# Sixteen row blocks of a down projection by seven block products in place of eight, with the weights' sums added up in DRAM by DMAs

## The chip, the cores and the metric

The kernel runs on one core of one Trainium2 chip. A core has five engines with an instruction stream each: TensorE (PE, the matmuls), VectorE (DVE), ScalarE (ACT), GpSimd (POOL) and SyncE (SP, which here issues nearly all DMAs), and 16 DMA engines that they share. The metric is the device time of one execution in microseconds (us).

## What is computed

One inference step of a hybrid layer for 512 prompt tokens (behind 16 meta tokens) and 8 x 8 sample tokens, with a model width of 1024. The end of it is what the change touches:

```python
def hybrid_layer(x, ...):
    proj = rmsnorm(x, norm1_w) @ w_in
    ...                                   # pooling mixer, conv, SSD scan, gated norm
    merged = sigmoid(g_a) * a_out + sigmoid(g_b) * b_out
    x = x + merged @ w_o
    hn2 = rmsnorm(x, norm2_w)
    up, ffn_new = causal_dwconv(hn2 @ w_up, ffn_buf, ffn_conv_w, ffn_conv_b)
    x = x + (silu(up[..., :D_FF]) * up[..., D_FF:]) @ w_down      # D_FF = 2816 = 22 * 128
    ...                                   # final rmsnorm, states
```

## The kernel before

Activations stand with features on the partitions and 576 tokens (512 and 64) along the row. Every product is one of fp32 numbers, made of three matmuls: a number is split in a high part (rounded to the fast format) and a low part (the rest), and `mm3` (L120 to L124) multiplies low weight by high activation, high by high, and high by low. Weights come by DMA (`load_w`, L95: 1 MB for two units of 128 output columns, two buffers `wr`); `split_w` makes the high part on ACT (L116) and the low part on DVE (L117), in two buffers `wh` and `wl` each.

A `Unit` is the product for 128 output columns: `split`, `product` (its matmuls into PSUM banks, three `mm` and five `px`) and `finish`, which calls the function that takes the result out. `run` goes through a list of units and splits the weights two units ahead. A scheduler then orders the instructions of each engine, so that their places are not those of the source.

The parts of the program, in order: input projection with pooling and conv (to some 190 us), the scan of the SSD mixer, woven with output products (to some 600 us), merge, the projection `w_o`, and the ConvFFN. In the scan each step loads rows of a cumulated sum from DRAM (`cumD`, L730), from which DVE makes decays (L733), and states (`state_ssm`, L814). SP issues these loads in turn with the weights' (L95), the gating rows (`gAD`, `mAD`, L625 and L629) and others. POOL clears and fills the edges of the conv's buffers (`ext`, L651 and L652; the pooling's, L544 and L545).

In the ConvFFN the 22 row blocks of the hidden width are made in pairs of units: a gate unit j and a value unit j. `ffn_conv` takes a unit out of PSUM (L1152 to L1154), convolves it (L1160 on ACT, L1162 twice on DVE); `gate_post` applies silu (L1174, L1175), `val_post` multiplies value by gate (L1185) and splits the product (L1189 on ACT, L1190 on POOL). One up unit has 48 matmuls. Units 0 to 11 are followed by `down0`, the down projection of these 12 row blocks: 8 units (128 output columns each) of 12 x 2 halves x 3 = 72 matmuls of 288 columns, added to x by DVE (L1215). Then units 12 to 21 and `last`, 8 units over 10 row blocks (60 matmuls each), woven with the output (`out_block`) and with 14 DMAs that write the FFN's states (L695).

```python
    down0 = down_units(0, [6, 6], GHALF)
    last = down_units(12, [8, 2], LAST)
    seq = up + down0 + ff_units(12, 10) + [out_begin, last[0]]
```

## Time and profile before

| | |
|---|---|
| median of 3 runs | 1235.24 us (1232.61 to 1235.53) |
| the profiled execution | 1235.61 us, span 1233.9 us |
| granted clock of TensorE | 0.996 of full speed |
| PE, DVE, ACT, POOL busy | 1216.6, 776.3, 556.0, 165.7 us |
| DMA traffic | 144.0 MB, mean 117 GB/s |

The span goes from the first to the last instruction of the profiled execution; 1.7 us of its time lie around it. Busy times are shares of this span; one engine's idle time matters only where PE waits for it.

### The profile page before, as it was taken

The page shows a single profiled execution, that of the slowest core. Times are in us where ns is not written, and L with a number is a line of the kernel's source. Part 1 is how long each engine was busy: PE and PEld are TensorE (multiplying, and loading weights), DVE is VectorE, ACT ScalarE, POOL GpSimd, SP SyncE. Part 2 cuts the span into 40 slices and gives each one's busy share as a digit, 9 for nine tenths or more (in the row PEclk, how much of TensorE's full clock was granted, in tenths as well). Part 3 has the DMA queues.
Part 4 walks back from the last instruction along what each step waited for, and adds up shares of the span by engine and source line. Part 5 has one row for each costly group of instructions (what it writes and reads, how often), then busy time and mean ns, then how long its engine had stood idle before and what let it go on. Part 6 is the DMA issues. An engine that isn't in the chain of part 4 may idle for free.

```text
span 1233.9 us, 22634 instructions
## 1 busy us (share of the span) xinstructions
PE 1216.6 (99%) x9159; PEld 1178.2 (95%) x9159; DVE 776.3 (63%) x1378; ACT 556.0 (45%) x1167; POOL 165.7 (13%) x323
## 2 busy tenths in 40 slices
PE   9999999999999999999999999999999999999996
PEld 7999999899899989989999999999999999999996
DVE  6785346669788988887643344377666325677634
ACT  6444333554567577566442224344434112434432
POOL 0340000002023013011100001221212000111100
PEclk9999999999999999999999999999999999999999
DMA  7244327651634555654553532223322223222322
GB/s 209 55 135 118 107 88 214 165 169 46 188 112 122 149 151 142 192 150 132 152 146 106 173 132 71 68 70 103 103 69 78 78 86 103 69 69 88 111 72 77
DMA packets 173432, 144.00 MB, mean 117 GB/s; under 512 B 11622, under 2 KB 162830, under 8 KB 173321
## 3 DMA queue, kind: packets, MB, share of 16 engines
q1 hardware_dynamic: 172865, 142.14, 39.4%
q8 instruction: 72, 1.18, 0.4%
q10 hardware_dynamic: 464, 0.42, 0.1%
q14 instruction: 31, 0.25, 0.1%
HBM read 122.43 MB, written 20.34 MB: 116 GB/s over the span
## 4 chain that ended last, share of the span: by engine, by line
PE 89%; DMA 4%; DVE 3%; ACT 2%; issue 1%; SPq 0%; POOL 0%; DVEq 0%; ACTq 0%; POOLq 0%
PE mm L122 26%; PE mm L123 26%; PE mm L124 26%; DMA t<-cumD 2%; PE px L785 1%; DMA t<-in_state_ssm_dram 1%; PE px L763 1%; PE px L794 1%; PE px L825 1%; DMA wr<-in_w_in_dram 1%; PE px L878 1%; PE px L838 1%; ACT t L735 1%; PE px L747 1%; DVE wl L117 1%
## 5 line engine op out<-in xcount | busy, mean ns | idle before, releaser
L122 PE MATMUL mm<-s,wl 128*128 128x288 f32 (+4 forms) x2512 | 754.9, 301 | 1.1 <-DVE wl L117 0.6
L123 PE MATMUL mm<-s,wh 128*128 128x288 f32 (+4 forms) x2512 | 746.8, 297 | 0.0
L124 PE MATMUL mm<-s,wh 128*128 128x288 f32 (+4 forms) x2256 | 671.8, 298 | 0.0
L122 PEld LDWEIGHTS mm<-s,wl 128*128 128x128 f32 x2512 | 473.8, 189 | 7.7 <-issue 5.3
L123 PEld LDWEIGHTS mm<-s,wh 128*128 128x128 f32 x2512 | 473.6, 189 | 3.6 <-issue 3.0
L124 PEld LDWEIGHTS mm<-s,wh 128*128 128x128 f32 x2256 | 424.6, 188 | 1.5 <-issue 1.4
L117 DVE TENSOR_TENSOR wl<-wr,wh 128x1024 fp32r<-128x1024 f32 (+1 forms) x164 | 197.9, 1207 | 167.0 <-ACT wh L116 166.5
L116 ACT ACTIVATE wh<-wr 128x1024 fp32r<-128x1024 f32 (+1 forms) x164 | 170.0, 1037 | 233.9 <-PE mm L124 197.1
L124 PE MATMUL mm<-t,wh 128*128 128x290 f32 (+1 forms) x256 | 75.9, 297 | 0.0
L1162 DVE SCALAR_TENSOR_TENSOR acc<-ext,ffT,acc 128x592 f32<-128x592 f32 x88 | 74.2, 844 | 1.7 <-ACT acc L1160 0.2
L663 DVE SCALAR_TENSOR_TENSOR acc<-ext,scT,acc 128x616 f32<-128x616 f32 x72 | 63.8, 886 | 0.9 <-ACT acc L661 0.4
L735 ACT ACTIVATE t<-t,TK 128x128 f32<-128x128 f32 (+1 forms) x160 | 48.4, 384 | 24.4 <-DVE t L733 24.4
L947 POOL TENSOR_TENSOR sqs<-sqs,acc 128x578 f32<-128x578 f32 x19 | 31.3, 1647 | 140.5 <-ACT acc L946 75.3
L124 PEld LDWEIGHTS mm<-t,wh 128*128 128x128 f32 x256 | 48.2, 188 | 0.0
L1189 ACT ACTIVATE s<-ext 128x512 fp32r<-128x512 f32 (+1 forms) x44 | 17.1, 436 | 64.3 <-DVE ext L1185 64.3
L882 ACT ACTIVATE t<-t,spr 128x128 f32<-128x128 f32 x128 | 40.3, 393 | 8.4 <-PE px L825 8.3
L1153 DVE TENSOR_TENSOR ext<-mm,t 128x224 f32<-128x224 f32 x43 | 16.8, 391 | 42.0 <-PE mm L124 42.0
L804 POOL TENSOR_TENSOR s<-s,tmp 128x256 f32<-128x256 f32 (+1 forms) x32 | 35.5, 1129 | 54.8 <-DVE tmp L798 47.2
L1190 POOL TENSOR_TENSOR s<-ext,s 128x512 fp32r<-128x512 f32 (+1 forms) x44 | 37.4, 870 | 35.1 <-ACT s L1189 35.1
L1215 DVE TENSOR_TENSOR t<-t,mm 128x288 f32<-128x288 f32 (+2 forms) x30 | 13.6, 452 | 43.8 <-PE mm L124 43.6
L1160 ACT ACTIVATE acc<-ext,ffT 128x592 f32<-128x592 f32 x44 | 38.2, 870 | 1.6 <-DVE ext L1154 1.6
L1156 POOL COPY t<-ext 128x18 f32<-128x18 f32 x44 | 11.4, 258 | 203.1 <-DVE ext L1154 203.0
(292 smaller groups left out, 1289.5 us busy)
## 6 DMA issues: line engine op xcount, KB each, us to landing
wr<-in_w_in_dram SPq DMA_DIRECT2D x29, 1024.0 KB
wr<-in_w_up_dram SPq DMA_DIRECT2D x22, 1024.0 KB
t<-cumD SPq DMA_DIRECT2D x16, 512.0 KB
t<-in_state_ssm_dram SPq DMA_DIRECT2D x32, 256.0 KB
out_dram<-t SPq DMA_DIRECT2D x32, 256.0 KB
wr<-in_w_ssd_out_dram SPq DMA_DIRECT2D x8, 1024.0 KB
wr<-in_w_down_dram SPq DMA_DIRECT2D x8, 768.0 KB
wr<-in_w_down_dram SPq DMA_DIRECT2D x8, 640.0 KB
```

Of the source, the lines that this page charges most:

```text
L116: S.activation(wh[:, :kb, :n], wr, AF.Copy)
L117: V.tensor_tensor(wl[:, :kb, :n], wr, f(wh[:, :kb, :n]), ALU.subtract)
L122: PE.matmul(o, wl[:, k, :m], hi[:, a:b], start=first, stop=False)
L123: PE.matmul(o, wh[:, k, :m], hi[:, a:b], start=False, stop=False)
L124: PE.matmul(o, wh[:, k, :m], lo[:, a:b], start=False, stop=last)
L663: V.scalar_tensor_tensor(acc[:, 0:616], ext[:, k:k + 616], scT[:, kb, 24 + k:25 + k], acc[:, 0:616], op0=ALU.mult, op1=ALU.add)
L735: S.activation(seg[:q, h, :q], seg[:q, h, :q], AF.Exp, scale=-1.0, bias=sums_[:, h:h + 1])
L804: G.tensor_tensor(v, v, t1[:, 2 * i:2 * i + 2, :nt], ALU.add)
L882: S.activation(v[:, b], v[:, b], AF.Copy, scale=elS[:, 4 * u + 2 * i + b, 4 * g + j:4 * g + j + 1])
L1160: S.activation(acc[:, 0:w], ext[:, 0:w], AF.Identity, scale=ffT[:, kb, 16:17], bias=ffT[:, kb, 19:20])
L1162: V.scalar_tensor_tensor(acc[:, 0:w], ext[:, k:k + w], ffT[:, kb, 16 + k:17 + k], acc[:, 0:w], op0=ALU.mult, op1=ALU.add)
L1190: G.tensor_tensor(l, a, f(h), ALU.subtract)
```

## The change

Row blocks 0 to 15 of `w_down` are taken in two groups of eight. In a group, the row blocks are read as four even and four odd ones, the output columns as two halves of four blocks each, and the tokens as two halves of 288. That is a 2 x 2 by 2 x 2 product of blocks, made by seven products (Winograd's form of Strassen's method) in place of eight. Four of the seven take sums of weight blocks, S1 to S4, and four take differences of the gated rows, N1, N2, T3 and T4.

`Sums` makes S1 to S4 of each group in DRAM: four DMAs on SP (L196) copy a block of the weights, [4, 128, 512] of 1 MB, and seven DMAs on POOL (L202) add another one to it. In the source they are woven into the merge (group 0) and the up projection (group 1). `Parts` loads the weights of four products (4 x 256 KB, L225). A `Two` is a unit of two products, 2 x 4 x 3 = 24 matmuls of 288 columns each, with one px bank a product; a group is 14 of them. `seven_post` adds a product to its one, two or three places in x. `val_post` makes the differences and their parts for every second row block below 16. The value rows' scale `rs2` moves to another buffer. Row blocks 16 to 21 stay in `last`, with 36 matmuls a unit. The first up unit of the next group now stands between the group's last value unit and its first `Two`.

```diff
--- before.py
+++ after.py
@@ -139,7 +139,7 @@
                 wr = self.raw() if callable(self.raw) else load_w(*self.raw)
                 self.ws, k0 = [], 0
                 for kb in self.kbs:
-                    w = split_w(wr[:, k0:k0 + kb, self.at:self.at + self.n], kb, self.n, self.spare if kb == 2 else None)
+                    w = split_w(wr[:, k0:k0 + kb, self.at:self.at + self.n], kb, self.n, self.spare if kb <= 2 else None)
                     self.ws += [(w, k) for k in range(kb)]
                     k0 += kb
                 self.pss = []
@@ -174,6 +174,106 @@
             else:
                 self.post(self.pss)
             due[:0] = [fn() for fn in now]
+    SEVEN = (("A11", "B11"), ("A12", "B21"), ("S4", "B22"), ("S2", "N2"), ("S1", "N1"), ("S3", "T3"), ("A22", "T4"))
+    class Sums:
+        def __init__(self, src, k0, name):
+            rows = src[k0 * 128:(k0 + 8) * 128, :].rearrange("(k e p) c -> e k p c", e=2, p=128)
+            self.at = {f"A{i + 1}{e + 1}": rows[e][:, :, 512 * i:512 * i + 512] for i in range(2) for e in range(2)}
+            self.d = {s: dp.tile([4, 128, 512], F32, name=f"{name}{s}") for s in ("S1", "S2", "S3", "S4")}
+        def copies(self):
+            def go(s, a):
+                return lambda: DMA.dma_start(out=self.d[s], in_=self.at[a])
+            return [go("S4", "A12"), go("S2", "A11"), go("S1", "A21"), go("S3", "A11")]
+        def adds(self):
+            def go(s, a):
+                return lambda: G.dma_start(out=self.d[s], in_=self.at[a], accum_op=ALU.add)
+            return [go("S4", "A11"), go("S2", "A21"), go("S1", "A22"), go("S3", "A21"), go("S4", "A21"), go("S2", "A22"), go("S4", "A22")]
+        def steps(self):
+            c, a = self.copies(), self.adds()
+            return [c[0], c[1], a[0], c[2], a[1], c[3], a[4], a[2], a[5], a[3], a[6]]
+        def view(self, name, mp):
+            full = self.d[name] if name in self.d else self.at[name]
+            return full.rearrange("k p c -> p k c")[:, :, 128 * mp:128 * mp + 128]
+    class Parts:
+        def __init__(self, views):
+            self.views, self.of, self.nxt = views, None, None
+        def load(self):
+            if self.of is None:
+                raws.clear()
+                self.of = wp.tile([128, 4, 4, 128], F32, tag="wr", bufs=2, name=nm("wr"))
+                for i, v in enumerate(self.views):
+                    DMA.dma_start(out=self.of[:, i], in_=v)
+        def get(self, i):
+            self.load()
+            if self.nxt:
+                self.nxt.load()
+            return self.of[:, i]
+    class Two(Unit):
+        def __init__(self, prods):
+            Unit.__init__(self, None, 0, None, None, None, None)
+            self.prods = prods
+        def split(self):
+            if self.ws is None:
+                self.ws = []
+                wh = wp.tile([128, 2, 4, 128], F32R, tag="wh", bufs=WBUFS, name=nm("wh"))
+                wl = wp.tile([128, 2, 4, 128], F32R, tag="wl", bufs=WBUFS, name=nm("wl"))
+                for i, (parts, at, *_) in enumerate(self.prods):
+                    src, n = parts.get(at), 4
+                    S.activation(wh[:, i, :n], src, AF.Copy)
+                    V.tensor_tensor(wl[:, i, :n], src, f(wh[:, i, :n]), ALU.subtract)
+                    self.ws.append(((wh[:, i], wl[:, i]), n))
+        def product(self, halves=None, piece=None):
+            for (_, _, acts, post), (w, n) in zip(self.prods, self.ws):
+                ps = px_tile()
+                for k in range(n):
+                    act = acts(k)
+                    n2 = act[0].shape[1]
+                    mm3(ps[:, :n2], w, k, 128, act, 0, n2, k == 0, k == n - 1)
+                post(ps)
+        def finish(self):
+            for fn in due:
+                fn()
+            due.clear()
+            now = pend[:]
+            pend.clear()
+            due[:0] = [fn() for fn in now]
+    def seven_units(sums, mps, acts, post):
+        todo = [(mp, w, x) for mp in mps for w, x in SEVEN]
+        parts = [Parts([sums.view(w, mp) for mp, w, _ in todo[i:i + 4]]) for i in range(0, len(todo), 4)]
+        for a, b in zip(parts, parts[1:]):
+            a.nxt = b
+        prods = [(parts[i // 4], i % 4, lambda k, x=x: acts(k)[x], lambda ps, mp=mp, w=w: post(mp, w, ps))
+                 for i, (mp, w, x) in enumerate(todo)]
+        return [Two(prods[i:i + 2]) for i in range(0, len(prods), 2)]
 
     def run(seq, nxt_units=()):
 
@@ -1131,14 +1231,17 @@
 
     o_units = mat_units(w_o_m, 0, [8], 2, lambda: [(blk(mh, k), blk(ml, k)) for k in range(KD)], ALIVE, o_post)
     o_units[0].k_outer = True
-    run(merge[:2] + [ff_params] + merge[2:] + [lambda: xr.extend(load_x(c) for c in range(5))], o_units)
-    x2s = []
+    dsum = [Sums(w_dn_m, 8 * i, f"w{i}") for i in range(2)]
+    run(merge[:2] + [ff_params] + weave(merge[2:], dsum[0].steps()) + [lambda: xr.extend(load_x(c) for c in range(5))], o_units)
+    x2s, rs2 = [], []
 
     def x2_norm():
-        return rnorm(sums["n2"], DM, lambda r, a, b: S.activation(rs2[:, a:b], r, AF.Copy))
-    nff, rs2 = slot([128, 18 * 44]), slot([128, NA])
+        spread = rnorm(sums["n2"], DM, lambda r, a, b: S.activation(rs2[0][:, a:b], r, AF.Copy))
+        rs2.append(ep.tile([128, NA], F32, tag="sqs", bufs=1, name=nm("sqs")))
+        return spread
+    nff = slot([128, 18 * 44])
 
     LF = LP - A0
     WF = LF + 8 * NB
...
@@ -1175,19 +1277,60 @@
         V.scalar_tensor_tensor(ext[:, 0:w], ext[:, 0:w], 1.0, acc[:, 0:w], op0=ALU.add, op1=ALU.mult)
         gates[j] = ext
 
+    NH = NY // 2
+    gB, quad = {}, {}
+    gh, gl = [], []
+    def split_g(hi, lo, src, eng):
+        S.activation(hi, src, AF.Copy)
+        eng.tensor_tensor(lo, src, f(hi), ALU.subtract)
     def val_post(j, pss):
-        if j % 2 == 0:
-            gh.extend(pairs(2, F32R))
-            gl.extend(pairs(2, F32R))
         _, acc, w = ffn_conv(NF + j, pss)
-        t = gates.pop(j)
-        for a, b in zip(parts(t), parts(acc)):
-            V.tensor_tensor(a, a, b, ALU.mult)
-        hi, lo = blk(gh, j)[:, :NY], blk(gl, j)[:, :NY]
-        for a, h, l in zip(parts(t), (hi[:, 0:NP], hi[:, NP:].rearrange("p (b j) -> p b j", b=NB)),
-                           (lo[:, 0:NP], lo[:, NP:].rearrange("p (b j) -> p b j", b=NB))):
-            S.activation(h, a, AF.Copy)
-            G.tensor_tensor(l, a, f(h), ALU.subtract)
+        t, p, e = gates.pop(j), j // 2, j % 2
+        if j >= 16:
...
+            return
+        if e == 0:
+            quad[p] = slot([128, 4, NH])
+        qd = quad[p]
+        g = qd[:, 2 * e:2 * e + 2].rearrange("p h t -> p (h t)")
+        for o, a, b in zip((g[:, 0:NP], g[:, NP:].rearrange("p (b j) -> p b j", b=NB)), parts(t), parts(acc)):
+            V.tensor_tensor(o, a, b, ALU.mult)
+        if e == 0:
+            new = slot if p % 4 == 3 else big
+            gB[p] = [new([128, 4, NH], F32R), new([128, 4, NH], F32R), big([128, 4, NH], F32R),
+                     gB[p - 1][3] if p % 2 else big([128, 4, NH], F32R)]
+            split_g(gB[p][2][:, 0], gB[p][2][:, 2], qd[:, 0], G)
+            return
+        del quad[p]
+        n1, n2 = t[:, 0:NH], t[:, NH:2 * NH]
+        t3, t4 = qd[:, 1], acc[:, 0:NH]
+        split_g(gB[p][0][:, 0:2], gB[p][1][:, 0:2], qd[:, 2:4], G)
+        V.tensor_tensor(n1, qd[:, 0], qd[:, 1], ALU.subtract)
+        V.scalar_tensor_tensor(n2, n1, -1.0, qd[:, 3], op0=ALU.mult, op1=ALU.subtract)
+        V.tensor_tensor(t3, qd[:, 3], qd[:, 1], ALU.subtract)
+        V.scalar_tensor_tensor(t4, n2, -1.0, qd[:, 2], op0=ALU.mult, op1=ALU.subtract)
+        split_g(gB[p][0][:, 2:4], gB[p][1][:, 2:4], t[:, 0:2 * NH].rearrange("p (h t) -> p h t", h=2), V)
+        split_g(gB[p][2][:, 1], gB[p][2][:, 3], t3, V)
+        i = 2 * (p % 2)
+        split_g(gB[p][3][:, i], gB[p][3][:, i + 1], t4, V)
+    def g_ops(p):
+        a, b, c, d = gB[p]
+        i = 2 * (p % 2)
+        return dict(B21=(a[:, 0], b[:, 0]), B22=(a[:, 1], b[:, 1]), N1=(a[:, 2], b[:, 2]), N2=(a[:, 3], b[:, 3]),
+                    B11=(c[:, 0], c[:, 2]), T3=(c[:, 1], c[:, 3]), T4=(d[:, i], d[:, i + 1]))
 
     def ff_units(j0, nj):
         out = []
@@ -1254,20 +1397,53 @@
             if q < n:
                 S.dma_start(out=o_ys.rearrange("b j d -> (b j) d"), in_=y[q:n, :])
 
-    def down_units(j0, kbs, halves):
-        return mat_units(w_dn_m, j0, kbs, 1, lambda: [(blk(gh, j0 + k), blk(gl, j0 + k)) for k in range(sum(kbs))], halves,
+    held = {}
+    def seven_post(mp, w, ps):
+        def to(c, src, op):
+            o = blk(x2, mp + 4 * (c // 2))[:, NMETA + NH * (c % 2):NMETA + NH * (c % 2) + NH]
+            V.tensor_tensor(o, o, src, op)
+        p = ps[:, :NH]
+        if w == "A11":
+            u = held["u"] = acc_tile()[:, :NH]
+            S.activation(u, p, AF.Copy)
+            to(0, p, ALU.add)
+        elif w == "S2":
+            u = held["u"]
+            V.tensor_tensor(u, u, p, ALU.add)
+            to(2, u, ALU.subtract)
+        elif w == "S1":
+            u = held.pop("u")
+            V.tensor_tensor(u, u, p, ALU.add)
+            to(1, u, ALU.add)
+            to(3, u, ALU.subtract)
+        elif w == "S3":
+            to(2, p, ALU.subtract)
+            to(3, p, ALU.subtract)
+        else:
+            c = {"A22": 2, "S4": 1, "A12": 0}[w]
+            to(c, p, ALU.subtract if c == 2 else ALU.add)
+    def down_sevens(i):
+        return seven_units(dsum[i], range(4), lambda k: g_ops(4 * i + k), seven_post)
+    def down_units(kbs, halves):
+        return mat_units(w_dn_m, 16, kbs, 1, lambda: [(blk(gh, k), blk(gl, k)) for k in range(6)], halves,
                          lambda m, pss: down_post(m, halves, pss))
 
-    up = ff_units(0, 12)
+    up = ff_units(0, 8)
     x_turn(0)
     run(o_units, up)
     x2s += [(blk(x2h, k), blk(x2l, k)) for k in range(KD)]
     pend.append(x2_norm)
     up[0].late, up[1].new, up[0].k_outer = True, px_tile, True
-    down0 = down_units(0, [6, 6], GHALF)
-    last = down_units(12, [8, 2], LAST)
+    up2, up3 = ff_units(8, 8), ff_units(16, 6)
+    last = down_units([5, 1], LAST)
     last[0].mate, last[1].mates, last[1].new = last[1], True, px_tile
-    seq = up + down0 + ff_units(12, 10) + [out_begin, last[0]]
+    seq = (weave(up, dsum[1].steps()) + up2[:1] + down_sevens(0) + up2[1:] + up3[:1] + down_sevens(1) + up3[1:]
+           + [out_begin, last[0]])
     for m in range(1, 6):
         seq += [last[m], *([ff_states] if m == 2 else []), lambda m=m: out_block(0, m - 1), lambda m=m: out_block(1, m - 1)]
     run(seq, last[6:])
```

Where the scheduler puts the DMAs of the sums is seen on SP and POOL. First SP, before, at the start of the scan, around the load of cumD into t310 (`wr` are weights, t308 and t309 states):

```order
L629 DMA mAD_139<-ext294_2356 128x578
L95 DMA wr330_2651<-in_w_pool_out_dram 128x8x256
L814 DMA t308_2464<-in_state_ssm_dram 128x4x128 x2
L814 DMA t309_2467<-in_state_ssm_dram 128x4x128 x2
L629 DMA mAD_139<-ext304_2453 128x578
L730 DMA t310_2470<-cumD_118 128x1024
L625 DMA ext329_2646<-gAD_140 128x578
```

The same place now; w1S1 is the second group's S1:

```order
L729 DMA mAD_139<-ext294_2356 128x578
L196 DMA w1S1_7486<-in_w_down_dram 512x1x512
L729 DMA mAD_139<-ext304_2453 128x578
L914 DMA t308_2464<-in_state_ssm_dram 128x4x128 x2
L914 DMA t309_2467<-in_state_ssm_dram 128x4x128 x2
L830 DMA t310_2470<-cumD_118 128x1024
L729 DMA mAD_139<-ext317_2548 128x578
L725 DMA ext329_2646<-gAD_140 128x578
```

The copy w1S1 has come ahead of the states and of t310's cumD, and the weight load wr330 has gone behind them. The other seven copies stand on SP between the early weight loads and the next step of the scan.

On POOL, before, in the pooling and the first conv buffers:

```order
L544 MEMSET ext133_1002 128x15
L545 COPY ext133_1002<-t19_113 128x8x15
L550 COPY t20_138<-ext133_1002 128x15
L551 COPY t20_138<-ext133_1002 128x64
L544 MEMSET ext150_1098 128x15
L545 COPY ext150_1098<-t19_113 128x8x15
L550 COPY t20_138<-ext150_1098 128x15
L551 COPY t20_138<-ext150_1098 128x64
L651 MEMSET ext161_1175 128x3
L652 COPY ext161_1175<-scT_115 128x8x3
```

And now:

```order
L644 MEMSET ext133_1002 128x15
L645 COPY ext133_1002<-t19_113 128x8x15
L202 DMA w0S4_7485<-in_w_down_dram 512x1x512
L650 COPY t20_138<-ext133_1002 128x15
L651 COPY t20_138<-ext133_1002 128x64
L644 MEMSET ext150_1098 128x15
L645 COPY ext150_1098<-t19_113 128x8x15
L650 COPY t20_138<-ext150_1098 128x15
L651 COPY t20_138<-ext150_1098 128x64
L202 DMA w0S4_7485<-in_w_down_dram 512x1x512
L751 MEMSET ext161_1175 128x3
L752 COPY ext161_1175<-scT_115 128x8x3
```

Two adds to w0S4 have come in between; the second waits for the first one's end, and ext161's clearing stands behind it. The other twelve follow further on, to the middle of the scan.

On DVE, before, behind the last value unit ahead of `down0`, from one split of `down0`'s weights (wl1309) to the next:

```order
L117 TENSOR_TENSOR wl1309_10742<-wr1305_10735,wh1308_10741 128x768
L1162 SCALAR_TENSOR_TENSOR acc1313_10801<-ext1312_10795,ffT_602,acc1313_10801 128x592 x2
L1185 TENSOR_TENSOR ext1303_10723<-ext1303_10723,acc1313_10801 128x512
L1185 TENSOR_TENSOR ext1303_10723<-ext1303_10723,acc1313_10801 128x8x8
L117 TENSOR_TENSOR wl1316_10814<-wr1314_10811,wh1315_10813 128x768
```

And now, where the first group of sevens begins, from the splits of the first `Two` (wl1267) on:

```order
L248 TENSOR_TENSOR wl1267_10315<-wr1268_10316,wh1266_10314 128x512 x2
L1265 SCALAR_TENSOR_TENSOR acc1265_10296<-ext1264_10290,ffT_602,acc1265_10296 128x592 x2
L1255 TENSOR_TENSOR ext1272_10381<-mm1270_10331,sqs1146_9204 128x290
L1308 TENSOR_TENSOR t1249_10158<-ext1257_10221,acc1265_10296 128x512
L1308 TENSOR_TENSOR t1249_10158<-ext1257_10221,acc1265_10296 128x64
L1319 TENSOR_TENSOR ext1257_10221<-t1249_10158 128x288
L1320 SCALAR_TENSOR_TENSOR ext1257_10221<-ext1257_10221,t1249_10158 128x288
L1321 TENSOR_TENSOR t1249_10158<-t1249_10158 128x288
L1322 SCALAR_TENSOR_TENSOR acc1265_10296<-ext1257_10221,t1249_10158 128x288
L1286 TENSOR_TENSOR t1251_10162<-ext1257_10221,t1250_10161 128x576
L1286 TENSOR_TENSOR s1252_10163<-t1249_10158,s1252_10163 128x288
L1286 TENSOR_TENSOR s1222_9875<-acc1265_10296,s1222_9875 128x288
```

Between the first `Two`'s splits and the next unit's stood the conv and the gating of a value unit, and now the differences (L1319 to L1322) and three low parts (L1286) besides. The rest of the evacuation (L1256, L1257) and the splits of the second `Two` (L248) come right behind.

## Rows read from the trace of the kernel before

**Rows 1.** The page's busy times of the engines.
```profile
PE 1216.6 (99%) x9159; PEld 1178.2 (95%) x9159; DVE 776.3 (63%) x1378; ACT 556.0 (45%) x1167; POOL 165.7 (13%) x323
```

**Rows 2.** Busy time by stretch; columns: from:to, length, engines, granted clock, DMA share, GB/s.
```profile
970.00:975.00 5.00, 5.00 (x40) 5.00 (x40) 0.96 (x1) 1.07 (x2) 0.00 (x0) 1.00 0.49 142
```

**Rows 3.** DVE's timeline, down projection: start, length, line, operation [idle before].
```profile
975.13 0.96 DVE L117 TENSOR_TENSOR wl<-wr,wh 128x768 fp32r<-128x768 f32 x1 [3.81 <-ACT wh L116]
984.68 0.96 DVE L117 TENSOR_TENSOR wl<-wr,wh 128x768 fp32r<-128x768 f32 x1 [3.81 <-ACT wh L116]
```

**Rows 4.** DVE's timeline and busy times over pairs of up projection units.
```profile
932.24 1.23 DVE L117 TENSOR_TENSOR wl<-wr,wh 128x1024 fp32r<-128x1024 f32 x1 [0.57 <-ACT wh L116]
933.39 1.70 DVE L1162 SCALAR_TENSOR_TENSOR acc<-ext,ffT,acc 128x592 f32<-128x592 f32 x2
937.56 0.39 DVE L1153 TENSOR_TENSOR ext<-mm,t 128x224 f32<-128x224 f32 x1 [0.84 <-PE mm L124]
938.65 1.23 DVE L117 TENSOR_TENSOR wl<-wr,wh 128x1024 fp32r<-128x1024 f32 x1 [0.57 <-ACT wh L116]
941.78 0.82 DVE L1185 TENSOR_TENSOR ext<-ext,acc 128x512 f32<-128x512 f32 x2
...
918.35:943.96 25.61, 25.61 (x194) 25.61 (x193) 17.82 (x30) 10.28 (x14) 4.66 (x13) 1.00 0.23 67
```

**Rows 5.** Groups by line and shape: busy time, mean ns of one, idle before.
```profile
L117 DVE TENSOR_TENSOR wl<-wr,wh 128x768 fp32r<-128x768 f32 x16 | 15.7, 978 | 28.0 <-ACT wh L116 28.0
L117 DVE TENSOR_TENSOR s<-wr,s 128x256 fp32r<-128x256 f32 x9 | 4.6, 506 | 11.8 <-ACT s L116 11.8
L1215 DVE TENSOR_TENSOR t<-t,mm 128x288 f32<-128x288 f32 x16 | 7.3, 454 | 19.0 <-PE mm L124 18.8
L1077 DVE TENSOR_TENSOR acc<-acc,ext 128x288 f32<-128x288 f32 x8 | 3.7, 460 | 0.3
```

**Rows 6.** DMA queues of the page: packets, MB, share of 16 engines.
```profile
q1 hardware_dynamic: 172865, 142.14, 39.4%
```

**Rows 7.** SP's timeline and stretches around the only DRAM to DRAM copy.
```profile
15.24 0.77 SPq L359 DMA_DIRECT2D out_dram<-in_state_pool_dram  x1
...
16.75:17.00 0.25, 0.25 (x5) 0.25 (x4) 0.25 (x1) 0.25 (x2) 0.00 (x0) 1.00 2.84 803
17.00:17.25 0.25, 0.25 (x4) 0.25 (x4) 0.25 (x1) 0.25 (x3) 0.00 (x0) 1.00 0.32 115
```

**Rows 8.** Busy time by stretch, the early part.
```profile
25.00:385.00 360.00, 355.62 (x2667) 341.27 (x2666) 243.10 (x411) 181.72 (x420) 51.40 (x115) 1.00 0.46 131
74.00:190.00 116.00, 116.00 (x862) 115.69 (x863) 58.24 (x84) 50.00 (x103) 6.18 (x25) 1.00 0.35 102
210.00:215.00 5.00, 5.00 (x40) 5.00 (x39) 2.43 (x5) 0.00 (x0) 0.00 (x0) 1.00 0.97 258
215.00:220.00 5.00, 3.93 (x39) 3.35 (x37) 3.46 (x6) 3.82 (x11) 0.00 (x0) 1.00 0.48 158
```

**Rows 9.** DVE's wait for cumD in its timeline, and all of them together.
```profile
214.92 1.23 DVE L733 TENSOR_TENSOR t<-t,TK 128x1024 f32<-128x1024 f32 x1 [2.13 <-DMA t<-cumD]
...
DVE t L733 <- DMA t<-cumD: 15.3, 10, 3.2
```

**Rows 10.** SP's timeline, loads of the scan.
```profile
202.98 3.41 SPq L814 DMA_DIRECT2D t<-in_state_ssm_dram  x4
209.29 0.38 SPq L730 DMA_DIRECT2D t<-cumD  x1
```

**Rows 11.** POOL's timeline, pooling and conv.
```profile
73.61 0.28 POOL L545 COPY ext<-t 128x120 f32<-128x120 f32 x1
87.58 0.10 POOL L651 MEMSET ext<- 128x3 f32 x1 [4.73 <-DVE ext L561]
```

**Rows 12.** SP's timeline near the end.
```profile
1179.74 9.38 SPq L695 DMA_DIRECT2D out_dram<-t  x14
1189.22 1.23 SPq L95 DMA_DIRECT2D wr<-in_w_down_dram  x2
```

More of the change, by code (lines that the diff above doesn't have):

```diff
@@ L1151, in ffn_conv @@
         G.tensor_copy(smp[:, :, 0:2], ffT[:, kb, 0:16].rearrange("p (b r) -> p b r", b=NB))
-        V.tensor_tensor(ext[:, 0:H0], pss[0][:, :H0], rs2[:, 0:H0], ALU.mult)
-        V.tensor_tensor(ext[:, H0:LF], pss[1][:, :LF - H0], rs2[:, H0:LF], ALU.mult)
+        V.tensor_tensor(ext[:, 0:H0], pss[0][:, :H0], rs2[0][:, 0:H0], ALU.mult)
+        V.tensor_tensor(ext[:, H0:LF], pss[1][:, :LF - H0], rs2[0][:, H0:LF], ALU.mult)
         V.tensor_tensor(smp[:, :, 2:10], pss[1][:, LF - H0:NA - H0].rearrange("p (b j) -> p b j", b=NB),
-                        rs2[:, LF:NA].rearrange("p (b j) -> p b j", b=NB), ALU.mult)
+                        rs2[0][:, LF:NA].rearrange("p (b j) -> p b j", b=NB), ALU.mult)
         G.tensor_copy(rows_at(nff, 18, 44, 7, kb),
@@ L1169, in hybrid_step @@
     gates = {}
-    gh, gl = [], []
     def gate_post(j, pss):
@@ L1186, in val_post @@
-        hi, lo = blk(gh, j)[:, :NY], blk(gl, j)[:, :NY]
-        for a, h, l in zip(parts(t), (hi[:, 0:NP], hi[:, NP:].rearrange("p (b j) -> p b j", b=NB)),
-                           (lo[:, 0:NP], lo[:, NP:].rearrange("p (b j) -> p b j", b=NB))):
-            S.activation(h, a, AF.Copy)
-            G.tensor_tensor(l, a, f(h), ALU.subtract)
+        t, p, e = gates.pop(j), j // 2, j % 2
+        if j >= 16:
+            if e == 0:
+                gh.extend(pairs(2, F32R))
+                gl.extend(pairs(2, F32R))
+            for a, b in zip(parts(t), parts(acc)):
+                V.tensor_tensor(a, a, b, ALU.mult)
+            hi, lo = blk(gh, j - 16)[:, :NY], blk(gl, j - 16)[:, :NY]
+            for a, h, l in zip(parts(t), (hi[:, 0:NP], hi[:, NP:].rearrange("p (b j) -> p b j", b=NB)),
+                               (lo[:, 0:NP], lo[:, NP:].rearrange("p (b j) -> p b j", b=NB))):
+                S.activation(h, a, AF.Copy)
+                G.tensor_tensor(l, a, f(h), ALU.subtract)
+            return
@@ new lines, in val_post @@
+        if e == 0:
[4 more added lines that the diff above has]
+            V.tensor_tensor(o, a, b, ALU.mult)
+        if e == 0:
+            new = slot if p % 4 == 3 else big
[3 more added lines that the diff above has]
+            return
```

## The prediction

> **What bounds the kernel now.** I read the page's busy times first. PE is busy in 1216.6 of 1233.9 us, so at most 17 us can be won by removing waits; more must come from fewer matmuls [rows 1]. Then the stretches of the down projection: PE is busy 5.00 of 5.00 us and DVE 0.96 there [rows 2]. In DVE's timeline the split of one unit's weights follows the last unit's by 9.55 us (975.13 to 984.68), and such a unit has 72 matmuls of 288 columns: 132.6 ns each [rows 3]. The reader sees a stage in which PE is the only limit, and DVE has much room.
>
> The up projection has less room: one unit of 48 matmuls lasts 6.41 us (932.24 to 938.65), and a gate unit with its value unit takes 8.92 of 12.81 us of DVE [rows 4]. The third place is far ahead, in the scan. There SP's loads are themselves waited for: DVE stands 15.3 us, in 10 waits, for cumD [rows 9].
>
> The profiled execution took 1235.61 us, 0.4 above the median; its span is 1233.9. I sum against 1235.6. About 0.3% (3.7 us) can be told from no change, so "the same" is 1231.5 to 1238.9.
>
> **Fewer matmuls.** Sixteen row blocks by eight column blocks by two halves by three passes were 768 matmuls of 288 columns. Seven products in place of eight make 672: 28 units of 24. The 96 that go are worth 96 x 132.6 ns = **-12.7 us**, if PE stays busy. The six row blocks that stay cost what they did.
>
> **Is PE still the limit in the seven products?** A new unit is 24 x 132.6 ns = 3.18 us. On DVE it has two weight splits of 512: no row has this size, and between 0.51 (256) and 0.98 us (768) I take 0.73. Per seven products the result is added in by 11 operations of 288, so 3.14 a unit at 0.45 us; the SBUF ones cost the same, 0.46 [rows 5]. That makes 1.46 + 1.42 = 2.88 us, 91% of the unit. It fits, with 0.30 us to spare; the heaviest unit (five adds, 3.7 us) is carried by the five px banks and its lighter neighbours. I cost it at nothing; if DVE is the limit after all, every 0.1 us above 3.18 costs 28 x 0.1 = 2.8 us.
>
> **Differences of the gated rows.** Every second value unit gets four subtractions of 288 and more low parts (one of 576, two of 288): 4 x 0.46 + 0.83 + 2 x 0.46 = 3.6 us more DVE. Two pairs have 17.8 of 25.6 us and would have 21.4, 84%: hidden under PE. But where a group of sevens begins, this load meets the first weight splits. DVE's order there is: the rest of the value unit's evacuation (0.39 and half of that for 64 columns, 0.6), the first unit's splits (1.46), the two steps of the conv (1.70), the next evacuation's first half (0.45, as one of 288), the gating (0.82) [rows 4], the differences (3.6), the rest of that evacuation (0.6), the second unit's splits (1.46): 10.7 us. PE's cover over this stretch is one up unit (6.4) and the first sevens unit (3.18), 9.6 us. So PE stands 1.1 us, perhaps twice; I take 1.5 at each of two places, **+3.0 us** (0 if the splits slip forward, 6.4 each if a whole unit is lost).
>
> **The end.** The last eight units shrink from 60 matmuls to 36, 8.0 to 4.8 us, while 14 state writes hold SP for 9.4 us and two loads stand behind them [rows 12]. Two short units nearly cover that: **+0.5 us**, 0 to 3.
>
> **The sums.** Here the order decides, not the source: the 8 copies and 14 adds, written beside the merge and the up projection, are issued between some 25 and 380 us (the times of their neighbours in the order, taken from the trace of before). They are first read near 900 us, so they can't be late; they can only be in the way.
> Price of a copy: the trace has 142.14 MB in 39.4% of 1233.9 us, 292 GB/s [rows 6], so 1 MB (1.05 million bytes) takes 3.6 us of all engines. The only DRAM to DRAM transfer, 224 KB, is issued from 15.24 to 16.01 and has moved by 17.25 us; 1.24 us for 224 KB is 5.7 for 1 MB [rows 7]. I take 3.6, the shape of the large loads, with 5.7 as the other end. No row shows an add. It reads twice and writes once: 3.6 (like a copy) to 7.2. All of them, 79 to 130 us of transfer in 360 us, lift a mean share of 0.46 to 0.68 or 0.82 [rows 8]. On the mean that fits.
> Ahead of the scan they are hidden: a weight load there is issued two units ahead of its split. At one place they are not. The copy w1S1 now stands on SP ahead of four loads of state_ssm and a cumD load. Before, these were issued from 202.98 and at 209.29 [rows 10]; the share was 0.97 in 210 to 215 and PE ran 3.93 of the next 5 us [rows 8]; DVE had waited 2.13 us for that cumD [rows 9]. Whatever delays this load goes to PE: one copy, **+3.6 us** (0 to 5.7).
> POOL's side: the second add into w0S4 waits for the first, and behind it stands the clearing of ext161. Before, POOL came to the first place at 73.9 us and cleared ext161 at 87.58 [rows 11]: 13.7 us of cover for an add of 3.6 to 7.2. Nothing. What issuing an add costs POOL is not in the trace; between SP's 0.38 us for a load and its 3.41 for four [rows 10] I take 1, on an engine that is 13% busy [rows 1].
>
> **Sum.** -12.7 + 3.0 + 0.5 + 3.6 = -5.6: 1230.0 against this execution, **1229.6** against the median.
>
> **Rivals.** *Four engines (slower).* The DMAs' outermost dimension is four blocks, and no load of before has that shape. If only four of sixteen engines carry them, 256 KB falls on each, at 292/16 = 18.3 GB/s: 14 us a copy, 14 to 29 an add. The first add then passes the 13.7 us of cover and POOL is late by 0 to 15 us; PE has about one unit of matmuls in hand (6.4 us) in its banks, so it loses 0 to 9. Loads behind w1S1 on those engines are late by up to 14 us, and 12 adds take half of four engines through the scan. Together 15 to 25 us early in place of 3.6: 1241 to 1251, I say **1246**. It decides from an early loss of 9.2 us on (12.7 - 3.5). Against it: the 224 KB copy has only eight outermost rows, and the two stretches of 0.25 us that hold its bytes show 803 and 115 GB/s [rows 7], far over what eight engines carry at that rate.
> The Trainium skill speaks for this rival. "DMA: Bandwidth & Descriptors", section "Why a DMA increments its semaphore by 16 and not by 1", says that a transfer uses the largest number of engines up to 16 that divides the slowest dimension of both patterns, four here, and "Rules for kernel authors" asks for a multiple of 16 outermost. By it the 14 us a copy holds, and the sum is 1246; by the rate of the rows it is 1229.6. No row of before shows the shape.
>
> *Nothing won (within 0.3%).* Sixteen engines, but the seven adds of the second group fall into the scan's ten waits for cumD. If each lengthens one by 0.5 to 1 us, 3.5 to 7 us more: 1233 to 1237, **1235**.
>
> *All hidden (faster by more).* The px and wl buffers absorb both transitions and the w1S1 copy overlaps: -12.7 + 0.5 to 1.5, **1223.5**. For it: between 74 and 190 us, where half of the copies go, PE is busy 116.00 of 116.00 us at a share of 0.35 [rows 8], so there is cover for more.
>
> **Chances.** Forecast 0.34, all hidden 0.13, nothing won 0.22, four engines 0.31. Faster by over 0.3%: 0.34 + 0.13 = 0.47; the same 0.22; slower 0.31. The likeliest case's own range is 1226 to 1231.5 (transitions 0 to 5, copy 0 to 5.7). For 8 in 10 the range runs from the all-hidden case to past the middle of the slow one: 1223 to 1248.
>
> **What would show it.** Right: in the sevens, weight splits in pairs every 3.18 us with PE 5.00 of 5.00, so some 89 us for 28 units; PE idle of 1 to 2 us at each group's first units; PE idle of 3 to 4 us more than before within 200 to 220 us; PE's matmul time down by 12.7. The four-engine rival shows as POOL waiting past 90 us ahead of ext161, and 10 us or more of idle PE between 75 and 260. The prediction is wrong if DVE is never idle in the sevens, if adds take over 13.7 us, or if the scan's waits for cumD grow from 15 us to over 25.

## The result, and the profile after

The changed kernel takes 1401.35 us (1397.52 to 1403.08), the kernel before 1234.84 in the same comparison: a ratio of 1.1346, 95% interval 1.1325 to 1.1368. It is slower by 13.5%, far outside the range. The page of the profiled execution, with its busy times (before: [rows 1]), the slices of PE and of the granted clock, and the new queue of the adds:

```profile
span 1399.4 us, 22857 instructions
PE 1252.6 (90%) x9063; PEld 1201.2 (86%) x9063; DVE 847.8 (61%) x1546; ACT 582.5 (42%) x1223; POOL 190.1 (14%) x321
PE   9972799799964769889999999999999999999997
PEclk9986789899977879999999999999999999999999
q0 software_dynamic: 28896, 14.85, 6.7%
w0S<-in_w_down_dram POOLq DMA_DIRECT2D x7, 1024.0 KB, 32.9
w1S<-in_w_down_dram POOLq DMA_DIRECT2D x7, 1024.0 KB, 28.5
```

The loss lies in the first half, where the copies and adds are, and not in the sevens. The adds of the two groups land 32.9 and 28.5 us after their issue, in the median. PE has fewer matmuls, yet is busy for longer, at a clock that is often below full. Some of the loss, by stretches (from:to, length, busy time of PE, its weight loads, DVE, ACT and POOL, granted clock, DMA share, GB/s):

```profile
70.00:75.00 5.00, 0.86 (x4) 0.69 (x4) 4.03 (x6) 3.64 (x7) 2.82 (x3) 0.50 0.16 18
75.00:80.00 5.00, 5.00 (x22) 5.00 (x22) 2.15 (x6) 1.06 (x4) 0.00 (x0) 0.52 0.83 187
80.00:85.00 5.00, 5.00 (x39) 5.00 (x38) 0.78 (x1) 1.78 (x4) 0.37 (x2) 1.00 0.34 79
110.00:145.00 35.00, 2.87 (x19) 2.64 (x19) 2.60 (x3) 3.81 (x13) 1.90 (x1) 0.61 0.67 159
```

PE stands for most of 70 to 75 us, and then runs 22 matmuls in 5 us at a clock of 0.52 (near 1.2 GHz) where it runs 39 at 1.00 (2.4 GHz) right after. In 110 to 145 it is busy for 2.87 of 35 us. What it waits for, from SP over DVE and ACT to PE (four timelines; start, length, line, operation, and in brackets the idle time before and what ended it):

```profile
111.00 1.03 SPq L95 DMA_DIRECT2D wr<-in_w_in_dram  x2
116.27 9.15 SPq L830 DMA_DIRECT2D t<-cumDt  x1
125.47 0.65 SPq L196 DMA_DIRECT2D w0S<-in_w_down_dram  x1
...
140.61 0.95 DVE L833 TENSOR_TENSOR t<-t,TK 96x768 f32<-96x768 f32 x1 [24.37 <-DMA t<-cumDt]
...
141.66 2.23 ACT L835 ACTIVATE t<-t,TK 96x96 f32<-96x96 f32 x8 [25.88 <-DVE t L833]
...
144.25 0.61 PE L122 MATMUL mm<-s,wl 128*128 128x288 f32 x1 [32.13 <-ACT ext L753]
```

The load of 288 KB into t (cumDt) is issued from 116.27 us, and DVE has its data at 140.6. Behind DVE's and ACT's waiting instructions stands the conv's evacuation (L753), which needs nothing of that load, and behind that PE for 32 us. POOL's adds, in its timeline, ran before and beside it:

```profile
71.20 2.06 POOL L202 DMA_DIRECT2D w0S<-in_w_down_dram  x1
103.20 1.91 POOL L202 DMA_DIRECT2D w0S<-in_w_down_dram  x1 [11.38 <-DMA w0S<-in_w_down_dram]
104.27 0.94 POOL L751 MEMSET ext<- 128x3 f32 x1
110.56 1.90 POOL L202 DMA_DIRECT2D w0S<-in_w_down_dram  x1 [4.15 <-DMA w0S<-in_w_down_dram]
```

POOL waited 11.4 us for the first add, and cleared ext161 at 104.27 us, not at 87.58 [rows 11]. The waits of all this, from the view of waits (total, times, longest; of before: [rows 9]):

```profile
DVE t L833 <- DMA t<-cumDt: 36.0, 2, 24.4
DVE t L833 <- DMA t<-cumD: 35.2, 7, 18.9
PE mm L122 <- ACT ext L753: 44.8, 7, 32.1
```

### The profile page after: what moved, and what is told of

Its sections match the earlier page's. It is cut to its first block, busy times and chain, and to the rows that moved or that the text cites. A ratio compares the mean times of both kernels' runs of the same rounds, so it can differ in the third digit from the quotient of the medians.

```text
span 1399.4 us, 22857 instructions
## 1 busy us (share of the span) xinstructions
PE 1252.6 (90%) x9063; PEld 1201.2 (86%) x9063; DVE 847.8 (61%) x1546; ACT 582.5 (42%) x1223; POOL 190.1 (14%) x321
## 4 chain that ended last, share of the span: by engine, by line
PE 65%; DMA 7%; DVE 6%; ACT 3%; issue 1%; SPq 0%; DVEq 0%; ACTq 0%
PE mm L122 17%; PE mm L123 17%; PE mm L124 17%; DMA t<-cumD 3%; PE px L122 2%; PE px L124 2%; PE px L123 2%; DMA t<-cumDt 2%; DMA wr<-in_w_in_dram 1%; PE px L863 1%; PE px L885 1%; PE px L894 1%; DMA t<-in_state_ssm_dram 1%; ACT t L982 1%; DVE wl L117 1%
## 5 line engine op out<-in xcount | busy, mean ns | idle before, releaser
L122 PE MATMUL mm<-s,wl 128*128 128x290 f32 (+4 forms) x2278 | 696.3, 306 | 82.3 <-ACT ext L753 44.8
L123 PE MATMUL mm<-s,wh 128*128 128x290 f32 (+4 forms) x2278 | 689.0, 302 | 0.0
L124 PE MATMUL mm<-s,wh 128*128 128x290 f32 (+3 forms) x2022 | 612.1, 303 | 0.0
L122 PEld LDWEIGHTS mm<-s,wl 128*128 128x128 f32 x2278 | 440.9, 194 | 91.6 <-ACT ext L753 47.7
L123 PEld LDWEIGHTS mm<-s,wh 128*128 128x128 f32 x2278 | 440.1, 193 | 2.5 <-issue 2.3
L124 PEld LDWEIGHTS mm<-s,wh 128*128 128x128 f32 x2022 | 390.7, 193 | 1.6 <-issue 1.5
L117 DVE TENSOR_TENSOR wl<-wr,wh 128x1024 fp32r<-128x1024 f32 (+1 forms) x148 | 178.3, 1207 | 194.7 <-ACT wh L116 194.4
L116 ACT ACTIVATE wh<-wr 128x1024 fp32r<-128x1024 f32 (+1 forms) x148 | 153.3, 1038 | 216.6 <-PE mm L124 161.9
L122 PE MATMUL px<-s,wl 128*128 128x288 f32 (+4 forms) x234 | 70.1, 300 | 1.2 <-DVE wl L248 1.1
L124 PE MATMUL px<-s,wh 128*128 128x288 f32 (+4 forms) x234 | 69.6, 297 | 0.0
L123 PE MATMUL px<-s,wh 128*128 128x288 f32 (+4 forms) x234 | 69.2, 296 | 0.0
L833 DVE TENSOR_TENSOR t<-t,TK 128x1024 f32<-128x1024 f32 (+1 forms) x20 | 23.3, 1164 | 71.2 <-DMA t<-cumDt 36.0
## 6 DMA issues: line engine op xcount, KB each, us to landing
w0S<-in_w_down_dram POOLq DMA_DIRECT2D x7, 1024.0 KB, 32.9
w1S<-in_w_down_dram POOLq DMA_DIRECT2D x7, 1024.0 KB, 28.5
```

The source lines that it names most:

```text
L116: S.activation(wh[:, :kb, :n], wr, AF.Copy)
L117: V.tensor_tensor(wl[:, :kb, :n], wr, f(wh[:, :kb, :n]), ALU.subtract)
L122: PE.matmul(o, wl[:, k, :m], hi[:, a:b], start=first, stop=False)
L123: PE.matmul(o, wh[:, k, :m], hi[:, a:b], start=False, stop=False)
L124: PE.matmul(o, wh[:, k, :m], lo[:, a:b], start=False, stop=last)
L833: V.tensor_tensor(sg, sg, sums_.unsqueeze(2).to_broadcast([q, 8, q]), ALU.max)
```

## The experiments

The theory after this result: a transfer with four blocks outermost runs on four of the sixteen DMA engines, so that it takes several times as long and holds back every load that has a part on these engines. Rivals: the volume (22 MB more in a part that has no room for it), the accumulating DMA itself (slow in any shape), or a loss in the sevens. The times stand beside 1233.6 to 1234.0 us for the kernel before in the same comparisons; single runs have no interval.

**1. Without the sums.** `steps` returns nothing, and the products read plain blocks:

```diff
-            return [c[0], c[1], a[0], c[2], a[1], c[3], a[4], a[2], a[5], a[3], a[6]]
+            return []
...
-            full = self.d[name] if name in self.d else self.at[name]
+            full = self.at[{"S4": "A12", "S2": "A11", "S1": "A21", "S3": "A11"}.get(name, name)]
```

> The changed kernel without the copies and adds: the seven products read plain weight blocks where S1 to S4 stood (so the sums are left out of the result), and everything else is as in the change. All theories that put the loss on the DMAs of the sums (four engines, volume, slow adds) expect it gone: the prediction's sum without its early term, -12.7 + 3.0 + 0.5, is 1226 us, 1222 to 1231. If the loss of 166 us stays (over 1300 us), it lies in the sevens or in how the scheduler moved other work.

1224.33 us, ratio 0.9923 (0.9908 to 0.9938). The whole loss comes with the DMAs of the sums (with the transfers, or with the order into which the scheduler puts other work beside them), and the rest of the change wins 9.3 us. Its page, stretches at the first group's begin and within it and at the second's begin, and DVE's timeline in the sevens:

```profile
PE 1205.0 (98%) x9063; PEld 1166.4 (95%) x9063; DVE 847.9 (69%) x1546; ACT 582.0 (48%) x1223; POOL 171.8 (14%) x307
```

```profile
900.00:920.00 20.00, 19.47 (x145) 19.02 (x144) 19.69 (x39) 10.10 (x19) 2.90 (x4) 1.00 0.37 103
918.00:928.00 10.00, 10.00 (x78) 10.00 (x77) 8.54 (x18) 3.76 (x7) 0.00 (x0) 1.00 0.60 170
1040.00:1060.00 20.00, 19.45 (x145) 19.01 (x144) 17.84 (x33) 10.57 (x17) 3.94 (x7) 1.00 0.36 102
```

```profile
919.45 1.29 DVE L248 TENSOR_TENSOR wl<-wr,wh 128x512 fp32r<-128x512 f32 x2
922.34 1.29 DVE L248 TENSOR_TENSOR wl<-wr,wh 128x512 fp32r<-128x512 f32 x2 [0.21 <-ACT wh L247]
926.10 1.29 DVE L248 TENSOR_TENSOR wl<-wr,wh 128x512 fp32r<-128x512 f32 x2
928.72 1.29 DVE L248 TENSOR_TENSOR wl<-wr,wh 128x512 fp32r<-128x512 f32 x2 [0.21 <-ACT wh L247]
```

In these stretches PE is busy throughout but for 0.53 and 0.55 us at the two begins. Weight splits come in pairs, 9.27 us for three units, 3.1 each, and DVE is 85% full there. Of the change's span of 1399.4 us against 1223.6 here, PE's idle time is 146.8 - 18.6 = 128.2 us and PE's busy time 1252.6 - 1205.0 = 47.6: the same matmuls at the lower clock.

**2. The prices by themselves.** In the kernel before, one chain of 1 MB transfers from and to DRAM that nothing reads, in the ConvFFN: a copy and two adds with four blocks outermost, then a copy and three adds with 128 rows outermost.

```diff
+        DMA.dma_start(out=pA, in_=A11)
+        G.dma_start(out=pA, in_=A12, accum_op=ALU.add)
+        G.dma_start(out=pA, in_=A12, accum_op=ALU.add)
+        DMA.dma_start(out=pB[0, 0:1, 0:16], in_=pA[0, 0:1, 0:16])
+        DMA.dma_start(out=pB.rearrange("k p c -> p k c"), in_=A11.rearrange("k p c -> p k c"))
+        G.dma_start(out=pB.rearrange("k p c -> p k c"), in_=A12.rearrange("k p c -> p k c"), accum_op=ALU.add)
...
```

> The kernel before, with one chain of transfers in the quiet down projection that feeds no output: a copy and two adds with four blocks outermost, then a copy and three adds with 128 rows outermost, 1 MB each. Four engines: copy 14 us or more and add 28 us in blocks; copy 3.6 to 6 us and add 4 to 8 us in rows. Slow adds: adds over 25 us in both shapes. Volume: all of them 4 to 8 us when they run alone. The time itself should stay at 1235 us, since nothing waits for them.

The issues with their landing, from the view of DMAs:

```profile
pB<-in_w_down_dram POOLq DMA_DIRECT2D x3, 1024.0 KB, 9.1
pA<-in_w_down_dram POOLq DMA_DIRECT2D x2, 1024.0 KB, 28.2
```

The trace's records of the 512 pieces of 2 KB of each transfer say how many engines carried it: the pieces' own times added up, by the time from the first to the last start.

```
                      first to last   sum of pieces   at a time
copy, four blocks        11.08 us        45.5 us          4.1
add,  four blocks        24.91 us        93.9 us          3.8
copy, 128 rows            4.33 us        63.0 us         14.5
add,  128 rows            6.61 us       105.0 us         15.9
```

Four engines is right, and an accumulating DMA as such is not slow: 6.6 us. The expectation that the time would stay was wrong: 1265.99 us (one run). A chain that nothing waits for cost 32 us, since loads and POOL's own work stood behind it. (A part may be the order: PE's longest wait there, 7.2 us, ends at 855.2, before the first add's issue.) A weight load met the first block add, and ACT waited for it to 883.9, where the add's last piece starts at 884.1; ACT's timeline:

```profile
883.90 1.06 ACT L116 ACTIVATE wh<-wr 128x1024 fp32r<-128x1024 f32 x1 [11.99 <-DMA wr<-in_w_up_dram]
```

**3. Rows outermost, where the scheduler wants them.** Copies and adds get `.rearrange("k p c -> p k c")` on both sides.

> The copies and adds name their 128 rows as the outermost dimension in place of the four blocks; same bytes, same pieces of 2 KB, same result. Four engines (the shape makes each transfer run on a quarter of the DMA engines): the transfers now take 4 to 8 us, the waits for cumDt and cumD shrink, 1228 to 1245 us. Volume (22 MB more in an early part that has no room): the shape makes no difference, over 1330 us. Slow adds (an accumulating DMA takes 25 us or more in any shape): adds still land after 25 us or more, over 1300 us.

1287.83 us, ratio 1.0439 (1.0422 to 1.0457): 113.5 us of the loss are gone and 63.5 over the kernel without sums stay, so neither theory holds alone. The scheduler now puts six copies into one piece; SP's timeline, and stretches:

```profile
25.73 7.98 SPq L196 DMA_DIRECT2D w0S<-in_w_down_dram  x4
33.76 5.83 SPq L196 DMA_DIRECT2D w1S<-in_w_down_dram  x2
...
80.00:90.00 10.00, 1.85 (x8) 0.95 (x7) 4.78 (x11) 1.63 (x2) 0.00 (x0) 0.68 1.10 260
90.00:100.00 10.00, 0.00 (x0) 0.00 (x0) 0.00 (x0) 0.00 (x0) 0.00 (x0) 0.50 1.10 234
```

At a share of 1.10 I read all sixteen engines as full (the records overlap a little). The adds land 21.4 and 16.7 us after their issue in the median, and PE's long wait behind the burst is one for weights; from the view of waits:

```profile
ACT t L116 <- DMA t<-in_pool_w_dram: 41.1, 1, 41.1
```

Here it is the volume at one time, and the order: on SP all eight copies now stand ahead of these loads.

**4. Rows outermost, late.** A tiny DMA from a late tile writes each sum's buffer first, and the sums move behind the output projection. In this run and in run 6 a few words of the sums can be overwritten by it.

```diff
+            for s in ("S4", "S2", "S1", "S3"):
+                DMA.dma_start(out=self.d[s][0, 0:1, 0:16], in_=src)
```

> Rows outermost as before, and each sum's buffer is first written by a tiny DMA from a tile of the late stage (x after the output projection; a gated row block), so that the copies and adds can't be issued before the up projection. Four engines and volume both expect the full gain less the transitions, 1222 to 1230 us, since up and sevens use a fifth to a third of the DMA engines. Slow adds: fourteen adds of 25 us or more on POOL hold its low parts of the gated rows, 1240 us or more.

1262.80 us, ratio 1.0237 (1.0219 to 1.0256). Four engines and volume both missed. The time lies where slow adds put it, 1240 us or more, but run 2 had such an add in 6.6 us by itself; here the adds land 20.0 and 19.5 us after their issue in the median, among the others. A later place is not enough, since the eleven transfers of a group still start as soon as they may. Over 860 to 880 us, and the wait for the up projection's weights:

```profile
860.00:880.00 20.00, 6.67 (x42) 6.47 (x41) 3.36 (x5) 2.53 (x3) 6.37 (x9) 0.73 1.11 234
...
ACT wh L116 <- DMA wr<-in_w_up_dram: 50.2, 6, 16.9
```

**5. The block-shaped copies alone**, in the early place: `steps` returns the copies only.

> The changed kernel with the eight block-shaped copies, early where the scheduler puts them, and without the adds (so S1 to S4 are one block each, and the sums are left out of the result). If the copies' hold on four engines is what delays the loads, some 20 to 60 us over the kernel without sums (1224): 1245 to 1285. If the adds do the harm (25 us each in the price run, against 11 for a copy), 1224 to 1232.

1288.14 us (one run), 63.8 over the kernel without sums; the other 113 come with the adds. The time is near what the first case expected, but the trace doesn't show its mechanism. The copies run one at a time, 21 to 54 us from start to start, and weight loads take hardly longer than in run 1 (the table after run 9); DVE's waits for cumD are shorter, 7.2 against 14.8 us. What has changed is SP's order. In run 1 three weight loads go out ahead of the pooling's output (L682):

```profile
71.70 26.84 SPq L95 DMA_DIRECT2D wr<-in_w_in_dram  x3
98.66 0.51 SPq L682 DMA_DIRECT2D out_dram<-t  x1
```

Here one does, then a copy, and the next two stand behind that output and two stores of gating rows. PE waits 9.1 us for the first of them:

```profile
75.40 0.37 SPq L95 DMA_DIRECT2D wr<-in_w_in_dram  x1
75.82 0.64 SPq L196 DMA_DIRECT2D w0S<-in_w_down_dram  x1
104.25 0.37 SPq L682 DMA_DIRECT2D out_dram<-t  x1
...
118.17 1.14 SPq L95 DMA_DIRECT2D wr<-in_w_in_dram  x2
...
128.23 0.61 PE L122 MATMUL mm<-s,wl 128*128 128x290 f32 x1 [9.11 <-DVE wl L117]
```

So the order that comes with the copies is the likelier cause of these 63.8 us; no run has the order without the copies.

**6. Four blocks outermost, late**: run 4 in the shape of the change.

> The same late placement as the pinned run with rows outermost (1263), but the transfers in the shape of the change, four blocks outermost. As there, a few words of the sums can be overwritten by the tiny DMAs that pin them. Four engines: fourteen adds of 25 us and eight copies of 11 us can't end by the time that the first sevens need them, and the weight loads of the up projection wait on the shared engines: 1300 us or more. Volume alone: the shape makes no difference, 1258 to 1268.

1339.16 us (one run), 76 over run 4. The shape costs there too.

**7. The sums on POOL in SBUF**, no DMAs of sums: four blocks are loaded once for seven products.

```diff
+                for o, x, y in (("S1", "A21", "A22"), ("S2", "S1", "A11"), ("S4", "S2", "A12"), ("S3", "A11", "A21")):
+                    G.tensor_tensor(self.of[o], self.of[x], self.of[y], ALU.add)
```

> No DMAs of sums: the four blocks of 128 columns are loaded once for seven products, and POOL adds S1 to S4 in SBUF (four operations of 512, some 4 us for each 11.1 us of products). If the loss of the change was the DMAs alone, this keeps what the run without sums showed, 1222 to 1228 us, with the full result. If POOL's adds slow DVE (91% full in the sevens) or come too late for the first products of a group, 1230 us or more.

1239.74 us, ratio 1.004 (1.0029 to 1.0052): 15.4 over the kernel without sums. DVE's weight splits, 684 ns there, now take (view of groups):

```profile
L227 DVE TENSOR_TENSOR wl<-wr,wh 128x512 fp32r<-128x512 f32 x32 | 33.3, 1066 | 1.0 <-ACT wh L226 0.8
L204 POOL TENSOR_TENSOR tmp<-tmp,wr 128x512 f32<-128x512 f32 x16 | 26.9, 1683 | 1.8 <-POOL tmp L204 1.4
```

DVE, 85% full in the sevens without them, is slowed by POOL's adds: the slow-DVE case of the expectation. PE's waits for these splits, all near the begins of the two groups:

```profile
PE px L122 <- DVE wl L227: 9.2, 8, 2.4
```

**8. One at a time.** Rows outermost; S2 is built on S1 and S4 on S2, so a group has four copies and four adds; and each is held back by a small chain through a tile of a certain unit (`mark`), meant as one every 12.8 us:

```diff
+                    S.activation(pb, mark, AF.Copy)
+                    S.dma_start(out=pb, in_=self.d[s][0, 0:1, 0:16])
+                    G.dma_start(out=rows(s), in_=rows(a), accum_op=ALU.add)
...
+            return [copy("S1", "A21"), add("S1", "A22"), copy("S2", "S1"), add("S2", "A11"), copy("S4", "S2"), add("S4", "A12"),
+                    copy("S3", "A11"), add("S3", "A21")]
```

> Eight transfers a group in place of eleven (S2 is built on S1 and S4 on S2), all with 128 rows outermost, and each held back by a small chain through a tile of a certain unit, so that one starts every 12.8 us from the output projection to the second up stage. Theory: what costs is transfers on few engines and in bursts; spread one by one over sixteen engines (4 us a copy, 6 to 8 an add) they hide, and the time is that without sums, 1222 to 1229 us. If any 16 MB of such traffic costs there, or the waits of POOL and ACT for it, 1235 us or more.

1223.60 us (1222.50 to 1227.14), ratio 0.9915 (0.990 to 0.993): the sums cost nothing, and this beats both kernels, by 10.4 us the one before. By name, all of DVE's operations, and ACT's but for those of the chains, stand in the order of run 1.

**9. One at a time, in blocks**: the same, without the rearrangement (copies from sum to sum are contiguous and keep their engines).

> The same held-back chain with the shape of the change: four blocks outermost in the copies from the weights and in all adds (copies from one sum to another are contiguous and keep sixteen engines). Four engines: eight adds of 25 us, each with weight loads behind it on its engines, 1250 to 1300 us. If spacing alone is what matters, 1222 to 1235, as with rows outermost.

1343.81 us (one run), 120 more, by the shape of four copies and eight adds and what the scheduler makes of it (1392 of DVE's 1546 operations stand in the order of run 8). An add now takes longer than the 12.8 us between two steps, so the adds meet. The waits for the weights of the up projection, in this run and in run 8:

```profile
ACT wh L116 <- DMA wr<-in_w_up_dram: 84.9, 10, 22.1
```

```profile
ACT wh L116 <- DMA wr<-in_w_up_dram: 5.7, 2, 2.9
```

That the shape does this to other loads is seen in the records of the 1 MB weight loads (1024 pieces of 1 KB), where one stands by itself:

```
                          loads   first to last start
before                     57     3.4 to 5.6 us
1, without sums            55     3.3 to 5.8
the change                 45     3.3 to 7.2, and 16.3 and 16.5
3, 128 rows, early         55     3.3 to 8.0, and 16.8 and 20.4
5, copies alone            52     3.3 to 6.3
8, 128 rows, spaced        57     3.2 to 5.8
9, four blocks, spaced     52     3.1 to 5.5, and four of 16.0 to 16.6
```

The two long ones of the change and the four of run 9 overlap a block add and have 3.2 to 3.7 pieces at a time, not 8 to 16. The two of run 3 stand in its burst.

All of them against the kernel without sums (1224.33 us; the kernel before differs by up to 1.2 us between the comparisons, so -0.7 is no difference):

| outermost | place | copies + adds | us | over |
|---|---|---|---|---|
| 4 blocks | early (the change) | 8 + 14 | 1401.35 | 177.0 |
| 4 blocks | early | 8 + 0 | 1288.14 | 63.8 |
| 4 blocks | late, at once | 8 + 14 | 1339.16 | 114.8 |
| 4 blocks | late, spaced | 8 + 8 | 1343.81 | 119.5 |
| 128 rows | early, at once | 8 + 14 | 1287.83 | 63.5 |
| 128 rows | late, at once | 8 + 14 | 1262.80 | 38.5 |
| 128 rows | late, spaced | 8 + 8 | 1223.60 | -0.7 |
| none | sums on POOL | 0 | 1239.74 | 15.4 |

## Why the prediction was wrong

**The step that failed** is the price of the sums, "+3.6 us (0 to 5.7)". It measured 1401.35 - 1224.33 = 177 us. Two things in it were wrong. First, "I take 3.6, the shape of the large loads": a copy of four blocks is not of that shape. It took 11.1 us on about four engines, an add 24.9. Second, "At one place they are not [hidden]": I followed one load, the cumD behind w1S1, and costed all others at nothing since the mean share had room. A mean over sixteen engines says nothing of four full ones. Weight loads that met an add took 16.3 and 16.5 us in the change, in place of 3.3 to 5.8, and the cumDt load between them landed 24 us after its issue.

**The four-engine rival** had the mechanism and the unit prices (14 us a copy, 14 to 29 an add), and the sign; but "15 to 25 us" for the early loss was too small by a factor of seven or more. I took the delays of two places. Run 5 points to a second cost, the scheduler's new order (64 us with the copies alone, where loads are hardly slower). The change shows that engines which issue in order pass one late load on to work that doesn't need it (the conv's evacuation behind the cumDt load), and that PE comes back at half clock: 47.6 of the 175.8 us.

**The evidence that I held against that rival was no evidence.** The 224 KB copy's "803 GB/s" came from a stretch whose share reads 2.84 [rows 7]: the view books a piece with all its bytes where it starts, so the row gives no rate. The records of the trace of before have the copy as eight pieces of 28 KB, begun between 16.78 and 17.07 us and ended by 18.59: eight at a time, 1.6 us and some 18 GB/s each, which is the rate per engine in the rival's own sum (18.3). So "has moved by 17.25 us" was a misreading too, and the copy spoke for the rival. The Trainium skill's "DMA: Bandwidth & Descriptors", section "Why a DMA increments its semaphore by 16 and not by 1", stood against it, and run 2 agrees with the page: 4.1 and 3.8 pieces at a time for four blocks, 14.5 and 15.9 for 128 rows.

**Volume in bursts** was no rival of mine as such; runs 3 and 4 show it: 63.5 and 38.5 us with sixteen engines in use (and another order of SP's DMAs), against nothing when the transfers are spaced (run 8, with 16 transfers in place of 22). My "on the mean that fits" was true, and not the question.

**What held.** The terms without the sums, -12.7 + 3.0 + 0.5 = -9.2 us, measured -9.3 (run 1). That it is so close is luck: PE's busy time fell by 11.6 us (predicted 12.7), and its idle time in the profiled executions grew by 1.3 (18.6 against 17.3; predicted 3.5). DVE did not become the limit. A transition cost less than my 1.5 us: PE's idle time at the two places is 0.53 and 0.55 us. POOL's cover of 13.7 us was the right test, and the add failed it: POOL came 16.7 us late. The signs that I had named came. For being wrong: an add over 13.7 us (24.9) and waits for cumD over 25 us (35.2). For four engines: POOL past 90 us ahead of ext161 (104.27).

**Open.** The sources of the 177 us weren't separated further. Shown are the price of the shape (run 2) and that it slows the loads beside it (run 9, and the two loads of the change); how much of the 177 us is this, and how much the scheduler's other order, is not. Run 5 points to the order for its 63.8 us, and the 113 us between it and the change hold the adds, their overlap with the copies, and a different order again.

## What to carry to other kernels

Price a DMA by the engines that its outermost dimension lets it use, and where the shape is new, measure one transfer before costing twenty. Off the path means that nothing reads it soon; whether it is harmless depends on what shares its engines and stands behind it, and on the peak, not on the mean share. A new DMA can also push others back in the order of its queue, so compare the order before and after as well. If a transfer may come late, hold it back by a true dependency and let one start at a time: 16 MB cost nothing so, and 120 us in the other shape.
